# A norm's square sums are added up on ScalarE instead of GpSimd in a two-layer decoder trunk

## The chip, the core and the metric

The kernel runs on one core of a Trainium2 chip. The metric is the device time of one execution in microseconds. In the profile's names PE is TensorE (matmuls), PEld its weight loads, ACT is ScalarE, DVE is VectorE, POOL is GpSimd, and SP the engine that issues most transfers. Every engine works through its own queue in order; they meet at semaphores.

## The reference

A decoder trunk of two layers over 256 positions of width 1024, in float32. Each layer has four sublayers: a SwiGLU feed-forward block, a mixer (layer 0: a chunkwise mLSTM; layer 1: differential attention over a shared K and V), a second feed-forward block, and a gated input embedding. Each is wrapped in RMS norms before and after:

```python
def rms_norm(x, g):
    y = x * lax.rsqrt(jnp.mean(x * x, axis=-1, keepdims=True) + EPS)
    return y * g

h = swiglu(rms_norm(x, g[0]), w_ffn_in[layer, 0], w_ffn_out[layer, 0])
x = x + 0.5 * rms_norm(h, g[1])
h = mixer(rms_norm(x, g[2]))
x = x + rms_norm(h, g[3])
h = swiglu(rms_norm(x, g[4]), w_ffn_in[layer, 1], w_ffn_out[layer, 1])
x = x + 0.5 * rms_norm(h, g[5])
gate = sigmoid(rms_norm(x, g[6]) @ w_ple_gate[layer])
x = x + rms_norm((p[layer] @ w_ple_proj[layer]) * gate, g[7])
```

The time goes into the weight matrices: all of them are read once, and each product is made of three float32r matmuls with operands that are split into a high and a low part.

## The kernel before

The 256 positions are two tiles of 128 rows, t = 0 and 1. x lives in SBUF with a copy in HBM. A weight tile of 128x2048 (buffers `wraw`) comes in through SP's queue, ScalarE rounds it to its high part (`whi`), and VectorE subtracts to get the low part (`wlo`). The same split makes `xh` and `xl` of the transposed x and `hh` and `hl` of the hidden activations. PSUM has three banks `accI` for the products of the inner width, four `accO` for those of the outer width, and one `tr` for transposes.

The trunk is not issued in the order in which it is written. `Notes.add` (L123) records every operation with its dependences and a cost (`cost`, L212), and `play` (L267) lays the whole program out by a list schedule with these costs: for each engine it takes the operation that can start first, urgent ones ahead of the splits of weights, and for TensorE transposes only when their input has been ready for a margin of 300 ns (MARGIN). `issue` (L430) then emits all operations in that order, so that in the profile nearly every instruction has line L433. In the costs a two-input VectorE operation holds GpSimd back until it ends (L404 to L407), a GpSimd addition is 321 ns, a power 560 ns, and an ACTIVATE of one column with a bias by pointer 163 ns. A change of a few operations therefore changes the order of many others.

A norm has these parts. `squares` (L565) runs an ACTIVATE Square over 512 columns (256 in two places of the last sublayer) whose accumulator gives one column of a small tile `s2` of four columns; an ACTIVATION_READ_ACCUMULATOR belongs to it. `rnorm` (L570) adds the columns of `s2` and eps with tensor_scalar operations on GpSimd and calls `rpow` (L557), which raises the sum to the power -0.5 by a GpSimd tensor_tensor with the constant tile `mhalf`. There are two uses of the result. Behind a sublayer, `post` (L600) and the end of `ple` (L951) hand it to `add_to_x` (L589): VectorE multiplies the sublayer's output by it and adds it to x, two halves of 512 columns, and TensorE then transposes the new x (`pre`, L682). Ahead of a sublayer, `rms_x` (L668) takes the norm of x, and the result scales the products where they leave PSUM, as in `hidden` (L805). There are 32 such norms of one column per tile of positions: 31 over two square sums, and the very last one over three. The mLSTM's and the attention's own head norms use `rpow` or the power alone and have no `rnorm`.

The small tiles of one column (`sm`, L452) rotate through eight buffers, the waste tiles of the squares (`sg`, L459) through three that hold hidden activations too.

Of the kernel before, what the change touches and what calls it, by code (L numbers as in the profile page):

```python
# [12 lines left out]
AF = mybir.ActivationFunctionType  # L13
ALU = mybir.AluOpType
# [9 lines left out]
EPS = 1e-6  # L24
# [411 lines left out]
def trunk(nc, a):  # L436
    def T(shape, tag, bufs, dt=F32):
        return nc.tile("sb", shape, tag, bufs, dt)
# [13 lines left out]
    def small(cols=1):  # L452
        return T([P, cols], f"sm{cols}", {1: 8, 2: 4, 4: 16}[cols])
# [87 lines left out]
    make_identity(nc, ident)  # L541
    mhalf = T([P, 8], "mhalf", 1)
    nc.gpsimd.memset(mhalf, -0.5)


    nc.scalar.activation(small(), mhalf[:, 0:1], AF.Silu)
# [10 lines left out]
    def rpow(v, cols=1):  # L557
        r = small(cols)
        nc.gpsimd.tensor_tensor(r, v, mhalf[:, :cols], op=ALU.pow)
        return r  # L560
# [7 lines left out]


    def rnorm(s2, n, coef):  # L570
        v = small()
        nc.gpsimd.tensor_scalar(v, s2[:, 0:1], s2[:, 1:2], EPS / coef ** 2, op0=ALU.add, op1=ALU.add)
        for i in range(2, n):
            v2 = small()
            nc.gpsimd.tensor_scalar(v2, v, s2[:, i:i + 1], None, op0=ALU.add)
            v = v2
        r = rpow(v)
        return r

    def rms(srcs, coef):  # L580
        s2 = small(4)
        for i, src in enumerate(srcs):
            squares(src, coef, s2, i)
        return rnorm(s2, 2, coef)
# [15 lines left out]
    def post(t, srcs, gbc, coef):  # L600
        gbc, hg = gbc
        s2 = small(4)
        for i in range(2):
            squares(srcs[i], coef, s2, i)
            j = 1 - i
            nc.vector.tensor_tensor(hg[:, halves[j]], srcs[j], gbc[:, halves[j]], op=ALU.mult)
        add_to_x(t, hg, rnorm(s2, 2, coef))
# [316 lines left out]
    def ple(l, xts, rs, epilogue):  # L924
# [26 lines left out]
        def end(t, n):  # L951
            r = rnorm(s2[t], n, 1.0)
            add_to_x(t, hg, r, store if epilogue is None else None)
            if epilogue is not None:
                res.append(epilogue(t))
# [466 lines left out]
@with_exitstack  # L1422
def issue(ctx: ExitStack, tc: tile.TileContext, plan, a):
    pools = {
        "sb": ctx.enter_context(tc.tile_pool(name="sb", bufs=1)),
        "dr": ctx.enter_context(tc.tile_pool(name="dr", bufs=1, space=bass.MemoryType.DRAM)),
        "ps": ctx.enter_context(tc.tile_pool(name="ps", bufs=1, space=bass.MemoryType.PSUM)),
    }
    notes = Notes(tc.nc, pools, plan)
    trunk(notes, a)  # L1430
    with tc.manual_schedule():
        notes.issue()
# [69 lines left out]
```

## Time and profile before

| what | us |
|---|---|
| timed runs, median of 3 | 1003.71 (1002.12 to 1003.89) |
| profiled execution, its own time | 1002.59 |
| its span, first to last instruction | 1000.8 |
| TensorE's mean granted clock | 0.997 |
| GpSimd: 32 tensor_scalar of one column, busy | 23.5 |
| GpSimd: 32 powers of one column, busy | 21.9 |
| ScalarE: idle in the span (1000.8 less 698.6 busy) | 302.2 |

A row of the timeline gives the start within the span, the duration, the engine, the operation, what it writes and reads, how many like it were merged, and in brackets the idle time of the engine before it with what ended that. A row of groups gives the count, busy time, mean duration in ns, and the idle time before. A row of waits gives the total, the count, and the longest. A row of windows gives, for one stretch, each engine's busy time with its count of instructions, then the TensorE clock, the share of the DMA engines, and the rate.

### The profile page before, as it was taken

The page shows a single profiled execution, that of the slowest core. Times are in us where ns is not written, and L with a number is a line of the kernel's source. Part 1 is how long each engine was busy: PE and PEld are TensorE (multiplying, and loading weights), DVE is VectorE, ACT ScalarE, POOL GpSimd, SP SyncE. Part 2 cuts the span into 40 slices and gives each one's busy share as a digit, 9 for nine tenths or more (in the row PEclk, how much of TensorE's full clock was granted, in tenths as well). Part 3 has the DMA queues.
Part 4 walks back from the last instruction along what each step waited for, and adds up shares of the span by engine and source line. Part 5 has one row for each costly group of instructions (what it writes and reads, how often), then busy time and mean ns, then how long its engine had stood idle before and what let it go on. Part 6 is the DMA issues. An engine that isn't in the chain of part 4 may idle for free.

```text
span 1000.8 us, 12442 instructions
## 1 busy us (share of the span) xinstructions
PE 986.4 (99%) x4636; PEld 803.0 (80%) x4636; DVE 892.8 (89%) x909; ACT 698.6 (70%) x924; POOL 94.9 (9%) x126
## 2 busy tenths in 40 slices
PE   9999999999999999999999999999999999999997
PEld 7888888887787778888878888888888887878786
DVE  6977999799999999998799999898984999999983
ACT  7746777578756877685867767686776776757752
POOL 0010000300141000001120000001002300000010
PEclk9999999999999999999999999999999999999998
DMA  9999948765699999765699999864759899996621
GB/s 345 420 339 343 311 179 296 244 207 198 255 320 340 326 309 335 279 247 207 261 301 330 324 353 347 329 244 161 253 210 285 235 297 318 313 295 252 242 84 43
DMA packets 45859, 274.68 MB, mean 274 GB/s; under 512 B 5480, under 2 KB 5864, under 8 KB 16104
## 3 DMA queue, kind: packets, MB, share of 16 engines
q1 hardware_dynamic: 39752, 231.69, 60.2%
q0 software_dynamic: 5760, 41.95, 20.6%
q8 instruction: 36, 0.59, 0.2%
q10 hardware_dynamic: 288, 0.27, 0.1%
q14 instruction: 23, 0.19, 0.1%
HBM read 263.40 MB, written 10.49 MB: 274 GB/s over the span
## 4 chain that ended last, share of the span: by engine, by line
PE 47%; issue 2%; ACT 2%; POOL 1%; DVE 1%; DVEq 0%; POOLq 0%; ACTq 0%
PE accI L433 30%; PE accO L433 15%; PE tr L433 2%; POOL sm L433 1%; ACT sg L433 1%; DVE wlo_4r L433 0%; ACT att L433 0%; DVE wlo_2r L433 0%; ACT wraw L433 0%; ACT whi_5r L433 0%; ACT whi_0r L433 0%; DVE wraw L433 0%; DVE att L433 0%; DVE xl_5r L433 0%; DVEq L1498 0%
## 5 line engine op out<-in xcount | busy, mean ns | idle before, releaser
L433 DVE TENSOR_TENSOR wraw<-wraw,wraw 128x2048 f32<-128x2048 f32 x40 | 91.4, 2284 | 0.1
L433 ACT ACTIVATE whi_1r<-wraw 128x2048 fp32r<-128x2048 f32 (+2 forms) x49 | 72.7, 1494 | 18.2 <-PE accI L433 8.8
L433 ACT ACTIVATE whi_4r<-wraw 128x2048 fp32r<-128x2048 f32 (+1 forms) x45 | 75.4, 1684 | 11.9 <-issue 4.4
L433 ACT ACTIVATE whi_2r<-wraw 128x2048 fp32r<-128x2048 f32 (+1 forms) x48 | 79.4, 1661 | 5.5 <-issue 2.6
L433 ACT ACTIVATE whi_5r<-wraw 128x2048 fp32r<-128x2048 f32 (+1 forms) x47 | 79.2, 1694 | 5.6 <-PE accI L433 4.7
L433 ACT ACTIVATE whi_0r<-wraw 128x2048 fp32r<-128x2048 f32 (+2 forms) x48 | 74.5, 1557 | 6.8 <-PE accI L433 3.4
L433 ACT ACTIVATE whi_3r<-wraw 128x2048 fp32r<-128x2048 f32 (+1 forms) x45 | 73.6, 1647 | 3.3 <-PE accI L433 1.6
L433 ACT ACTIVATE att<-accI 128x512 f32<-128x512 f32 x80 | 47.5, 594 | 38.1 <-PE accI L433 37.8
L433 POOL DMA_DIRECT2D wraw<-in_ffn_in x36 | 32.0, 889 | 343.5 <-DMA wraw<-in_ffn_in 286.3
L433 POOL TENSOR_SCALAR sm<-sm 128x1 f32<-128x1 f32 x32 | 23.5, 735 | 308.8 <-ACT sg L433 308.8
L433 POOL TENSOR_TENSOR sm<-sm,mhalf 128x1 f32<-128x1 f32 (+2 forms) x40 | 30.7, 769 | 108.2 <-DVE sm L433 105.6
L433 ACT ACTIVATE sg<-att,sm 128x256 f32<-128x256 f32 x54 | 26.9, 502 | 16.9 <-DVE att L433 16.8
L433 ACT ACTIVATE sg<-accO 128x512 bf16<-128x512 f32 (+2 forms) x46 | 20.2, 445 | 25.0 <-PE accO L433 21.0
L433 ACT ACTIVATE sg<-accI,sm 128x256 f32<-128x256 f32 x34 | 16.0, 470 | 29.3 <-PE accI L433 27.3
L433 PEld LDWEIGHTS tr<-ident,sg 128*128 128x128 f32 x176 | 23.0, 140 | 14.6 <-DVE hl_2r L433 2.7
L433 PE MATMUL tr<-ident,sg 128*128 128x128 f32 x176 | 34.0, 274 | 0.3 <-DVE hl_2r L433 0.3
L433 DVE SCALAR_TENSOR_TENSOR wraw<-wraw,sm,wraw 128x512 f32<-128x512 f32 x32 | 22.7, 749 | 12.0 <-POOL sm L433 11.9
L433 DVE TENSOR_TENSOR att<-accI,att 128x512 f32<-128x512 f32 x40 | 27.4, 685 | 3.3 <-PE accI L433 2.9
L433 ACT ACTIVATE sg<-wraw 128x512 bf16<-128x512 f32 x32 | 20.1, 630 | 13.7 <-DVE wraw L433 9.7
L433 ACT ACTIVATE att<-accI,sm 128x512 f32<-128x512 f32 (+1 forms) x22 | 14.8, 671 | 20.8 <-PE accI L433 20.8
L433 DVE SCALAR_TENSOR_TENSOR sg<-att,sm,sg 128x256 f32<-128x256 f32 x54 | 25.7, 480 | 1.7 <-ACT sg L433 1.5
L433 DVE TENSOR_TENSOR att<-att,att 128x512 f32<-128x512 f32 (+1 forms) x33 | 22.4, 679 | 3.8 <-ACT att L433 3.6
(610 smaller groups left out, 3249.9 us busy)
## 6 DMA issues: line engine op xcount, KB each, us to landing
wraw<-in_ffn_in SPq DMA_DIRECT2D x102, 1024.0 KB, 9.4
wraw<-in_ffn_out SPq DMA_DIRECT2D x44, 1024.0 KB, 8.3
wraw<-in_ffn_in POOLq DMA_DIRECT2D x36, 1024.0 KB, 13.3
wraw<-in_mlstm_in SPq DMA_DIRECT2D x14, 1024.0 KB, 5.3
wraw<-in_ple_gate SPq DMA_DIRECT2D x8, 1024.0 KB, 5.1
wraw<-in_w_kv SPq DMA_DIRECT2D x8, 1024.0 KB, 4.8
home<-wraw SPq DMA_DIRECT2D x28, 256.0 KB, 5.1
wraw<-home SPq DMA_DIRECT2D x14, 512.0 KB, 5.4
```

The costliest lines, as they stand in the source:

```text
L433: getattr(getattr(self.nc, eng), name)(*args, **kw)
```

## The change

`rnorm` no longer uses GpSimd for sums. Two columns of `mhalf` that no power reads, 6 and 7, are overwritten with eps for the two coefficients. The sum then starts from eps, and each column of `s2` is added by an ACTIVATE Identity on ScalarE whose bias is the sum so far. The power stays on GpSimd.

```diff
     mhalf = T([P, 8], "mhalf", 1)
     nc.gpsimd.memset(mhalf, -0.5)
+    eps = {coef: mhalf[:, c:c + 1] for c, coef in ((6, 1.0), (7, 0.5))}
+    for coef, v in eps.items():
+        nc.gpsimd.memset(v, EPS / coef ** 2)
...
     def rnorm(s2, n, coef):
-        v = small()
-        nc.gpsimd.tensor_scalar(v, s2[:, 0:1], s2[:, 1:2], EPS / coef ** 2, op0=ALU.add, op1=ALU.add)
-        for i in range(2, n):
+        v = eps[coef]
+        for i in range(n):
             v2 = small()
-            nc.gpsimd.tensor_scalar(v2, v, s2[:, i:i + 1], None, op0=ALU.add)
+            nc.scalar.activation(v2, s2[:, i:i + 1], AF.Identity, bias=v)
             v = v2
-        r = rpow(v)
-        return r
+        return rpow(v)
```

A norm over two square sums so has one GpSimd operation less and two ScalarE operations more, and three small tiles in place of two. Since the schedule is made anew, the order of the other instructions changes too. Three places follow.

ScalarE at the first norm, right behind the first weight tiles; `sg` with `sm_0` or `sm_1` are the squares of x for t = 0 and t = 1, `sg_128<-accI_90` is the SiLU of the first hidden tile, which reads the norm's result. Before:

```order
L433 ACTIVATE sg_127,sm_0_134<-wraw_80 128x512
L433 ACTIVATE sg_128,sm_0_134<-wraw_80 128x512
L433 ACTIVATE sg_126,sm_1_135<-wraw_80 128x512
L433 ACTIVATE sg_127,sm_1_135<-wraw_80 128x512
L433 ACTIVATE sg_128<-accI_90,sm_2_158 128x256
L433 ACTIVATE whi_3r<-wraw_81 128x1024
```

Of the change:

```order
L433 ACTIVATE sg_127,sm_0_134<-wraw_80 128x512
L433 ACTIVATE sg_128,sm_0_134<-wraw_80 128x512
L433 ACTIVATE sm_1_157<-sm_0_134,mhalf_133 128x1
L433 ACTIVATE sg_126,sm_1_135<-wraw_80 128x512
L433 ACTIVATE sm_2_158<-sm_0_134,sm_1_157 128x1
L433 ACTIVATE sg_127,sm_1_135<-wraw_80 128x512
L433 ACTIVATE sm_4_160<-sm_1_135,mhalf_133 128x1
L433 ACTIVATE sg_128<-accI_90,sm_3_159 128x256
L433 ACTIVATE sm_5_161<-sm_1_135,sm_4_160 128x1
L433 ACTIVATE whi_3r<-wraw_81 128x1024
```

The second addition for t = 0 stands behind the first square for t = 1, and with it the power that it feeds.

ScalarE behind the second feed-forward block of layer 0, t = 0 (465 us in the profile), where `sg` with `sm_0` are the two squares of the block's output in the banks `accO`. Before:

```order
L433 ACTIVATE hh_1r<-tr_97 128x256
L433 ACTIVATE sg_128,sm_0_134<-accO_96 128x512
L433 ACTIVATE sg_126,sm_0_134<-accO_94 128x512
L433 ACTIVATE whi_0r<-wraw_79 128x1024
L433 ACTIVATE sg_127,sm_1_135<-wraw_76 128x512
```

Of the change:

```order
L433 ACTIVATE hh_1r<-tr_97 128x256
L433 ACTIVATE sg_128,sm_0_134<-accO_96 128x512
L433 ACTIVATE sm_0_156<-sm_0_134,mhalf_133 128x1
L433 ACTIVATE sg_126,sm_0_134<-accO_94 128x512
L433 ACTIVATE sm_5_161<-sm_0_134,sm_0_156 128x1
L433 ACTIVATE whi_5r<-wraw_78 128x1024
L433 ACTIVATE sg_127,sm_1_135<-wraw_76 128x512
```

The first addition stands between the two squares, the second behind both. So it is at 14 of the 16 norms behind a sublayer; at the other two, behind the second feed-forward blocks at t = 1, the two additions follow both squares.

VectorE behind the mLSTM's output projection, t = 1 (293 us in the profile): the two products with the norm's gains, subtractions of large weight tiles (`wlo`), and the addition to x (`wraw_80<-wraw_81,sm`). Before:

```order
L433 TENSOR_TENSOR wraw_81<-accO_93,wraw_81 128x512
L433 TENSOR_TENSOR wraw_81<-accO_95,wraw_81 128x512
L433 TENSOR_TENSOR wlo_2r<-wraw_82,whi_5r 128x2048
L433 TENSOR_TENSOR wlo_4r<-wraw_84,whi_2r 128x2048
L433 SCALAR_TENSOR_TENSOR wraw_80<-wraw_81,sm_2_158,wraw_80 128x512 x2
L433 SCALAR_TENSOR_TENSOR sg_127<-accI_90,sm_1_157,sg_127 128x256
```

Of the change:

```order
L433 TENSOR_TENSOR wraw_81<-accO_93,wraw_81 128x512
L433 TENSOR_TENSOR wraw_81<-accO_95,wraw_81 128x512
L433 TENSOR_TENSOR wlo_2r<-wraw_82,whi_5r 128x2048
L433 SCALAR_TENSOR_TENSOR wraw_80<-wraw_81,sm_4_160,wraw_80 128x512 x2
L433 TENSOR_TENSOR att_103<-tr_97,gcol_130 128x512
L433 TENSOR_TENSOR att_99<-accI_91,gcol_130 128x512
```

The addition to x now stands ahead of the second large subtraction, and TensorE's transposes of that x stand ten rows earlier in its order. The same happens behind the first feed-forward block of layer 0 and behind the attention, both at t = 1.

## The prediction

> **What bounds the kernel now.** I read the busy line of the page first, then who waited for whom, then the stretches in which TensorE lost time, then the norms one by one.
>
> ```profile
> PE 986.4 (99%) x4636; PEld 803.0 (80%) x4636; DVE 892.8 (89%) x909; ACT 698.6 (70%) x924; POOL 94.9 (9%) x126
> DVE wraw L433 <- POOL sm L433: 17.3, 20, 1.2
> PE tr L433 <- DVE wraw L433: 0.7, 2, 0.4
> 300.00:320.00 20.00, 18.88 (x86) 14.33 (x85) 19.83 (x25) 16.16 (x22) 2.68 (x4) 1.00 1.03 328
> 314.15 0.50 PE L433 MATMUL accI<-wlo_4r,xh_2r 128*128 128x512 f32 x1 [0.65 <-DVE wlo_4r L433]
> 831.23 0.50 PE L433 MATMUL accI<-whi_0r,xh_2r 128*128 128x512 f32 x1 [1.06 <-ACT whi_0r L433]
> 832.76 0.50 PE L433 MATMUL accI<-wlo_2r,xh_5r 128*128 128x512 f32 x1 [1.03 <-DVE wlo_2r L433]
> ```
>
> TensorE is busy 986.4 of 1000.8 us, so all its idle time together is 14.4 us. VectorE waits 20 times, 17.3 us in all, for GpSimd's norm results before it adds a sublayer's output to x; but TensorE's transposes of that x waited for VectorE only twice, 0.7 us together. The norm chain is therefore almost wholly hidden. What TensorE loses in mid-kernel it loses elsewhere: in stretches behind a norm such as 300 to 320, where VectorE is busy 19.83 of 20 us and the weights' halves come late (the waits at 314.15, 831.23 and 832.76). A shorter norm chain can win little; a longer one costs only where its cover is thinner than what it grows by. So I look at the cover, place by place.
>
> **The change part by part.** It removes 33 tensor_scalar from GpSimd and adds 65 one-column ACTIVATEs to ScalarE, one for every square sum, so two for most of the 32 norms. The power on GpSimd stays. The two new memsets fall before 18.50, the first norm, up to which GpSimd has nothing to do (its row below shows 17.20 us idle). No DMA is added or removed, and the count of table loads on ScalarE is 11 in both orders.
>
> Prices:
>
> ```profile
> L433 POOL TENSOR_SCALAR sm<-sm x32: 293/302/4202, 18.5 to 992.1; 128x1 f32<-128x1 f32 x32
> L433 ACT ACTIVATE sm<-mhalf 128x1 f32<-128x1 f32 x1 | 0.2, 203 | 0.0
> L433 ACT ACTIVATE att<-accI 128x512 f32<-128x512 f32 x80 | 47.5, 594 | 38.1 <-PE accI L433 37.8
> L433 ACT ACTIVATE att<-accI,sm 128x512 f32<-128x512 f32 x20 | 13.8, 691 | 18.8 <-PE accI L433 18.7
> ```
>
> A removed sum costs 0.30 us at its median. A one-column ACTIVATE without an operand by pointer takes 0.20; a pointer operand adds 691 - 594 = 97 ns at 512 columns, so one new addition takes 0.20 + 0.10 = 0.30. The same duration on either engine: the difference lies in where it stands. It is at least 0.20, and 0.39 if the pointer's step counted twice; the row with a pointer is the nearer. The 65 additions are 65 x 0.30 = 20 us on an engine that is idle for 300, and cost nothing where nobody waits behind them.
>
> *The first norm.* It is computed before the first hidden tile can be formed.
>
> ```profile
> 18.21 0.19 ACT L433 ACTIVATION_READ_ACCUMULATOR sg<-wraw 128x1 f32 x1
> 18.43 0.63 ACT L433 ACTIVATE sg<-wraw 128x512 bf16<-128x512 f32 x1
> 18.50 0.30 POOL L433 TENSOR_SCALAR sm<-sm 128x1 f32<-128x1 f32 x1 [17.20 <-ACT sg L433]
> 18.89 0.57 POOL L433 TENSOR_TENSOR sm<-sm,mhalf 128x1 f32<-128x1 f32 x1
> 18.96 0.19 ACT L433 ACTIVATION_READ_ACCUMULATOR sg<-wraw 128x1 f32 x1
> 19.06 0.62 ACT L433 ACTIVATE sg<-wraw 128x512 bf16<-128x512 f32 x1
> 19.67 0.46 ACT L433 ACTIVATE sg<-accI,sm 128x256 f32<-128x256 f32 x1
> 20.70 0.50 PE L433 MATMUL accI<-whi_2r,xh_1r 128*128 128x512 f32 x1 [0.16 <-DVE sg L433]
> ```
>
> Today the sum runs on GpSimd while ScalarE already squares the second token tile. In the new order the second addition of tile 0 stands behind the first square of tile 1. ScalarE starts an instruction 0.09 before the one ahead ends (the read of 18.96 ends at 19.15, the next starts at 19.06). So, from the read that ends at 18.40: first addition 18.31 to 18.61; square 18.52; second addition one square step (18.43 to 19.06, 0.63) later, 19.15 to 19.45; 0.16 to reach GpSimd (the hop from 994.86 to 995.02 in the tail's rows); power 19.61 to 20.18. ScalarE has then done the last square and the third addition and starts the SiLU at about 20.28 instead of 19.67. The gated tile and TensorE's next use of the bank follow it at a fixed distance, and TensorE was already waiting for them at 20.70. I charge **+0.6 us**. The order puts nothing else there that TensorE could do meanwhile.
>
> *The norms behind a sublayer, GpSimd free.*
>
> ```profile
> 464.47 0.60 ACT L433 ACTIVATE sg<-accO 128x512 bf16<-128x512 f32 x1 [0.26 <-DVE wraw L433]
> 464.96 0.20 ACT L433 ACTIVATION_READ_ACCUMULATOR sg<-accO 128x1 f32 x1
> 465.26 0.30 POOL L433 TENSOR_SCALAR sm<-sm 128x1 f32<-128x1 f32 x1 [79.17 <-ACT sg L433]
> 465.64 0.56 POOL L433 TENSOR_TENSOR sm<-sm,mhalf 128x1 f32<-128x1 f32 x1
> 466.24 1.41 DVE L433 SCALAR_TENSOR_TENSOR wraw<-wraw,sm,wraw 128x512 f32<-128x512 f32 x2 [1.21 <-POOL sm L433]
> 467.63 0.60 PE L433 MATMUL tr<-ident,wraw 128*128 128x128 f32 x4
> 777.27 1.42 DVE L433 SCALAR_TENSOR_TENSOR wraw<-wraw,sm,wraw 128x512 f32<-128x512 f32 x2 [0.61 <-POOL sm L433]
> 778.62 0.60 PE L433 MATMUL tr<-ident,wraw 128*128 128x128 f32 x4
> ```
>
> The new order sets the first addition between the two squares, into the 0.26 us that ScalarE waits there anyway; only the second stays in the chain. A GpSimd instruction that depends on the one before it starts 0.08 after that one ends (465.56 to 465.64); with that hop on ScalarE too: 465.16 + 0.08 + 0.30 + 0.16 = 465.70 against 465.64, **0.06 us later**. The first half of x is done at 466.24 + 0.75 = 466.99 (1.41 for two that overlap by the same 0.09: 0.75 each), and the transpose starts at 467.63: a cover of 0.64, and 0.60 by the second pair (778.02 to 778.62). Behind it stand other matmuls that need not wait. Cost **0**; without that cover it would be 0.06 each at seven such places, 0.4. Two additions stand side by side at two places only, one of them the norm of 471.82 below; there the chain grows by 0.06 + 0.38 = 0.44, but its sum took 0.85 today, 0.55 more than it needs, so that again nothing is lost.
>
> *The norms behind a sublayer, GpSimd held.*
>
> ```profile
> 293.97 4.20 POOL L433 TENSOR_SCALAR sm<-sm 128x1 f32<-128x1 f32 x1 [5.03 <-ACT sg L433]
> 295.80 2.28 DVE L433 TENSOR_TENSOR wlo_4r<-wraw,whi_2r 128x2048 fp32r<-128x2048 f32 x1
> 298.85 1.42 DVE L433 SCALAR_TENSOR_TENSOR wraw<-wraw,sm,wraw 128x512 f32<-128x512 f32 x2 [0.77 <-POOL sm L433]
> 299.23 0.39 PE L433 MATMUL accI<-wlo_2r,xh_5r 128*128 128x512 f32 x1
> 299.66 0.55 PE L433 MATMUL tr<-ident,wraw 128*128 128x128 f32 x3
> 505.91 0.65 PE L433 MATMUL tr<-ident,wraw 128*128 128x128 f32 x4 [0.23 <-DVE wraw L433]
> 471.82 0.85 POOL L433 TENSOR_SCALAR sm<-sm 128x1 f32<-128x1 f32 x1 [2.22 <-ACT sg L433]
> 472.51 1.22 DVE L433 TENSOR_TENSOR wlo_3r<-wraw,whi_0r 128x1024 fp32r<-128x1024 f32 x1
> 472.76 1.39 POOL L433 TENSOR_TENSOR sm<-sm,mhalf 128x1 f32<-128x1 f32 x1
> 474.18 1.42 DVE L433 SCALAR_TENSOR_TENSOR wraw<-wraw,sm,wraw 128x512 f32<-128x512 f32 x2 [0.45 <-POOL sm L433]
> ```
>
> Here the sum of 0.30 took 4.20: it came while VectorE subtracted two large weight tiles, both operands in SBUF, and ended 0.09 after the second one did. The power then still had to run, so VectorE stood 0.77. Where the power itself was held (472.76) VectorE stood only 0.45. With the sum on ScalarE the power is what meets the subtraction: 0.77 - 0.45 = 0.3 us sooner. The new order moreover lets the addition to x pass in front of one of the large subtractions, so that x is complete a whole subtraction (2.2 us) sooner, and the transposes stand ten rows earlier on TensorE; they meet x at about the same distance as now. TensorE lost 0.20 at 299.66 (a step of 0.43, where a matmul takes 0.23) and 0.23 at 505.91: 0.43 to be had at most, below that a loss of as much if the transposes now come too early. I take half as a gain, **-0.2 us**, since the 0.3 is nearer to removing a wait of 0.2 than to adding one.
>
> The Trainium skill (SBUF — State Buffer, "Who interferes with whom") says that the loser of the shared port between VectorE and GpSimd blocks until the other's instruction ends, with DVE-end + about 115 ns given for a descriptor write under "A bandwidth-pool intuition that's wrong". The 4.20 us row agrees with 0.09; the held power does not, it ended 0.42 after VectorE did (474.15 against 473.73). By the page the gain would be 0.3 more at each such norm and the term -0.4; by the row, -0.2. The same rule speaks against the change: the lock is not removed, only handed from the sum to the power.
>
> *The tail.*
>
> ```profile
> 994.67 0.19 ACT L433 ACTIVATION_READ_ACCUMULATOR sg<-att 128x1 f32 x1
> 995.02 0.29 POOL L433 TENSOR_SCALAR sm<-sm,sm 128x1 f32<-128x1 f32 x1 [2.64 <-ACT sg L433]
> 995.40 0.56 POOL L433 TENSOR_TENSOR sm<-sm,mhalf 128x1 f32<-128x1 f32 x1
> ```
>
> Nothing hides this one. Of its three additions only the last comes behind the last square: 994.86 + 0.08 + 0.30 + 0.16 = 995.40, where the power starts today: **0**, between -0.1 (no hop inside ScalarE) and +0.1 (a hop of 0.16 there).
>
> *Sum:* +0.6 + 0 - 0.2 + 0 = **+0.4 us**. The profiled execution took 1002.59 (span 1000.8 and 1.79 around it), so 1003.0 for one like it. The timed median, 1003.71, lies 1.12 above; the same +0.4 on it gives **1004.1**, inside what the measurement can tell from no change, about 0.2% or 2 us.
>
> **The rivals.**
>
> *Slower, VectorE kept waiting in front of a norm.* With the addition to x set ahead of a large subtraction, VectorE, which now fills that time with the subtraction, stands idle until the power is done, 0.45 by the row of 472.76 and up to 0.77 by that of 298.85. In stretches like that of 300 to 320 the weights then come later by as much, and TensorE waits at places like 314.15 and 832.76. At four such norms: 4 x 0.6 = 2.4, with the first norm's 0.6 1003.71 + 3.0 = 1006.7. It decides where VectorE's new idle time exceeds the 0.77 that it stood already; that today's wait is as long speaks against it.
>
> *Slower, the dependent addition waits long on its own engine.* No row shows ScalarE waiting for its own result. GpSimd's own hop is 0.08; 0.16 is the hop between engines. Each norm has two, so the chain grows by twice what lies above 0.08, and at the free norms it decides at a hop of 0.08 + 0.54 / 2 = 0.35. At 0.5 a chain grows by 0.84: 7 x 0.3 behind the cover, 0.8 at the first norm and 0.4 in the tail, 1004.1 + 3.3 = 1007.4. Two kinds of hop below 0.2 speak against it.
>
> *Faster, the held norms open up the busy stretches.* If x 2.2 us sooner lets TensorE fill the waits behind it, 0.43 + 0.65 + 1.06 + 1.03 = 3.2 go: 1003.71 + 0.6 - 3.2 = 1001.1. Against it: those waits are for subtractions and splits, whose number is unchanged.
>
> *The change does nothing:* excluded, the new order shows the additions.
>
> **How the numbers follow.** Forecast 0.60; VectorE waiting 0.16; own-engine hop 0.08; faster 0.16. The range runs from the faster case, 1001, to the slower ones, **1000.8 to 1007.5**; the re-laid plan moves thousands of TensorE rows by a place or two, which these ends also have to cover. Faster by over 0.2% (below 1001.7) 0.16, within 0.61, slower (above 1005.7) 0.23; the forecast's own spread is 1002.6 to 1005.6.
>
> **What would show it.** The wait of TensorE for the first hidden tile near 20.7 should grow to about 0.8 and everything behind it shift. Post norms should show one addition of 0.30 between the squares, VectorE's wait near 1.2 as before at free norms and 0.45 at held ones. If TensorE's transposes of x wait more than 0.7 in all, the cover was misread; if the waits at 314 and 831 to 833 gain or lose over 1 us, VectorE decided and not the chain. A new addition far from 0.30, or a gap over 0.35 between two, makes the prediction wrong.

## The result, and the profile after

| | us |
|---|---|
| kernel before, median of 4 runs beside it | 1003.06 (1002.12 to 1003.89) |
| changed kernel, median of 4 runs | 1010.33 (1008.17 to 1011.62) |
| ratio, 95% interval | 1.0073 (1.0059 to 1.0087) |
| predicted | 1004.1, range 1000.8 to 1007.5 |
| profiled execution of the changed kernel: time, span, mean granted clock | 1008.17, 1006.4, 0.998 |

The change costs 7.3 us, and the range did not hold it. The profiled execution is the shortest of the four, so its trace shows some 5.6 us of the loss; the rest comes up below (the clock).

Little of it is at the norms. First the page and the list of waits of the changed kernel (waits: total, count, longest).

```profile
PE 987.5 (98%) x4636; PEld 802.9 (80%) x4636; DVE 894.3 (89%) x909; ACT 713.7 (71%) x989; POOL 77.4 (8%) x95
DVE wraw L433 <- POOL sm L433: 16.3, 22, 1.2
PE tr L433 <- DVE wraw L433: 0.4, 1, 0.4
```

VectorE's waits for norm results went from 17.3 to 16.3 us, TensorE's for the new x from 0.7 to 0.4. Now the new additions by group, and a norm with GpSimd free, one with it held, and the tail, from the timeline of the changed kernel.

```profile
L433 ACT ACTIVATE sm<-sm,sm x33: 278/294/297, 18.9 to 1001.0; 128x1 f32<-128x1 f32 x33
L433 ACT ACTIVATE sm<-sm,mhalf x32: 278/284/296, 18.1 to 996.0; 128x1 f32<-128x1 f32 x32
```

```profile
467.79 0.20 ACT L433 ACTIVATION_READ_ACCUMULATOR sg<-accO 128x1 f32 x1
468.02 0.29 ACT L433 ACTIVATE sm<-sm,sm 128x1 f32<-128x1 f32 x1
468.46 0.56 POOL L433 TENSOR_TENSOR sm<-sm,mhalf 128x1 f32<-128x1 f32 x1 [81.03 <-ACT sm L433]
469.06 1.42 DVE L433 SCALAR_TENSOR_TENSOR wraw<-wraw,sm,wraw 128x512 f32<-128x512 f32 x2 [1.20 <-POOL sm L433]
470.23 0.60 PE L433 MATMUL tr<-ident,wraw 128*128 128x128 f32 x4
...
293.76 2.28 DVE L433 TENSOR_TENSOR wlo_2r<-wraw,whi_5r 128x2048 fp32r<-128x2048 f32 x1
294.37 2.08 POOL L433 TENSOR_TENSOR sm<-sm,mhalf 128x1 f32<-128x1 f32 x1 [6.67 <-ACT sm L433]
296.48 1.42 DVE L433 SCALAR_TENSOR_TENSOR wraw<-wraw,sm,wraw 128x512 f32<-128x512 f32 x2 [0.44 <-POOL sm L433]
297.34 0.60 PE L433 MATMUL tr<-ident,wraw 128*128 128x128 f32 x4
...
1000.78 0.19 ACT L433 ACTIVATION_READ_ACCUMULATOR sg<-att 128x1 f32 x1
1000.99 0.29 ACT L433 ACTIVATE sm<-sm,sm 128x1 f32<-128x1 f32 x1
1001.37 0.55 POOL L433 TENSOR_TENSOR sm<-sm,mhalf 128x1 f32<-128x1 f32 x1 [9.88 <-ACT sm L433]
```

An addition takes 0.28 to 0.30. It starts 0.02 to 0.03 after the end of the read that it depends on. At the free norm VectorE waits 1.20 (1.21 before) and x is done 0.42 ahead of its transpose; at the held one VectorE waits 0.44 (0.77 before); in the tail 0.40 pass from the read's end to the power, where 0.54 passed.

One cost at a norm remains, at the first. Here are the first square of x and the first SiLU that reads the norm, in the kernel before (its SiLU starts at 19.67 and the next matmul on that bank at 20.70, as the prediction's rows show) and in the changed one.

```profile
17.06 0.63 ACT L433 ACTIVATE sg<-wraw 128x512 bf16<-128x512 f32 x1 [0.22 <-DMA wraw<-in_x]
```

```profile
16.86 0.63 ACT L433 ACTIVATE sg<-wraw 128x512 bf16<-128x512 f32 x1 [0.22 <-DMA wraw<-in_x]
...
19.89 0.45 ACT L433 ACTIVATE sg<-accI,sm 128x256 f32<-128x256 f32 x1
```

From the square to the SiLU it is 2.61 before and 3.03 after: the additions cost 0.42 there.

The rest of the loss shows in TensorE's waits behind the norms, in the feed-forward blocks. Here are the large ones from the timeline of the changed kernel (the first row, 20.91, is the first norm's), then windows of before and of after (busy time of PE, PEld, DVE, ACT, POOL with counts, then TensorE's clock, the DMA share, GB/s).

```profile
20.91 0.50 PE L433 MATMUL accI<-whi_2r,xh_1r 128*128 128x512 f32 x1 [0.88 <-DVE sg L433]
314.50 0.50 PE L433 MATMUL accI<-wlo_3r,xh_2r 128*128 128x512 f32 x1 [0.83 <-DVE wlo_3r L433]
354.18 0.49 PE L433 MATMUL accI<-whi_3r,xh_5r 128*128 128x512 f32 x1 [1.24 <-ACT whi_3r L433]
355.10 0.50 PE L433 MATMUL accI<-wlo_2r,xh_0r 128*128 128x512 f32 x1 [0.42 <-DVE wlo_2r L433]
534.93 0.50 PE L433 MATMUL accI<-wlo_0r,xh_6r 128*128 128x512 f32 x1 [2.48 <-DVE wlo_0r L433]
838.14 0.50 PE L433 MATMUL accI<-whi_4r,xh_2r 128*128 128x512 f32 x1 [0.98 <-ACT whi_4r L433]
839.17 0.50 PE L433 MATMUL accI<-wlo_2r,xh_5r 128*128 128x512 f32 x1 [0.53 <-DVE wlo_2r L433]
```

```profile
340.00:360.00 20.00, 19.38 (x85) 15.17 (x84) 20.00 (x17) 13.07 (x14) 1.72 (x2) 1.00 0.96 329
520.00:540.00 20.00, 20.00 (x92) 16.34 (x91) 19.55 (x18) 12.15 (x12) 1.76 (x2) 1.00 1.00 367
```

```profile
340.00:360.00 20.00, 17.87 (x76) 13.51 (x75) 19.40 (x14) 14.30 (x15) 1.73 (x2) 1.00 0.95 317
520.00:540.00 20.00, 17.52 (x82) 14.03 (x81) 17.87 (x18) 10.05 (x11) 1.76 (x2) 1.00 1.01 398
```

In each of two stretches of 20 us TensorE does some ten matmuls fewer, waiting for weights (`whi`, `wlo`) that come late. The same can be read as a lag: how much later (us) the n-th matmul starts than the n-th of the kernel before, in the profiled executions (e1 to e9 are the experiments below; the 4636 matmuls are numbered in order of time, from 0).

```
n      before  after     e1     e2     e3     e4     e5     e6     e7     e8     e9
60       16.7  -0.50  -0.50  +1.04  -0.19  -0.41  -0.13  -0.31  -0.16  -0.36  -0.29
300      70.0  +0.19  -0.20  +1.11  -0.01  +0.10  +0.25  -0.15  -0.11  -0.04  +0.73
1200    261.2  +0.19  -0.17  +0.98  +0.10  -0.16  +0.08  -0.01  +0.16  -0.01  +8.29
1620    356.5  +2.86  +2.54  +1.00  -0.03  +2.17  -0.11  -0.19  +0.08  +2.67  +8.23
2400    526.1  +2.11  +2.24  +1.50  -0.76  +2.10  -0.36  -0.43  -0.38  +1.93  +8.46
2460    539.6  +4.84  +6.50  +1.50  +3.50  +2.13  -0.34  -0.40  +4.01  +2.44  +8.46
3120    685.9  +5.37  +7.24  +1.59  +3.66  +2.13  -0.37  -0.39  +4.26  +2.97  +8.42
3240    709.3  +6.67  +8.55  +1.50  +4.99  +2.10  +0.81  -1.39  +5.52  +4.25  +8.54
3720    792.7  +5.80  +8.09  +1.49  +4.16  +2.08  -0.01  -0.07  +4.69  +3.40 +10.47
3960    848.5  +6.42 +10.30  +4.08  +4.81  +3.66  +2.29  -0.11  +5.35  +4.14 +12.16
4635    993.1  +6.10  +9.90  +4.04  +4.39  +3.25  +1.91  -0.37  +4.93  +3.71 +11.80
```

Column "after": next to nothing until 261 us, 2.7 at about 350, 0.8 won back by 526, 2.7 at 535, and 1.3 in all behind that. The first row lies ahead of the first norm (18.5 us), so what stands there (1.04 in e2) is not the additions' doing.

### The profile page after: what moved, and what is told of

The parts are those of the page before. It is cut to its first block, busy times and chain, and to the rows that moved or that the text cites. A ratio compares the mean times of both kernels' runs of the same rounds, so it can differ in the third digit from the quotient of the medians.

```text
span 1006.4 us, 12473 instructions
## 1 busy us (share of the span) xinstructions
PE 987.5 (98%) x4636; PEld 802.9 (80%) x4636; DVE 894.3 (89%) x909; ACT 713.7 (71%) x989; POOL 77.4 (8%) x95
## 4 chain that ended last, share of the span: by engine, by line
PE 83%; DVE 6%; DMA 4%; ACT 3%; issue 2%; POOL 1%; SPq 0%; DVEq 0%; POOLq 0%; ACTq 0%
PE accI L433 49%; PE accO L433 30%; PE tr L433 4%; DMA wraw<-in_ffn_in 2%; DVE wraw L433 1%; DMA wraw<-in_mlstm_in 1%; ACT sg L433 1%; DVE att L433 1%; DVE wlo_2r L433 1%; DMA wraw<-in_x 1%; DVE wlo_0r L433 1%; POOL sm L433 1%; DVE wlo_3r L433 1%; DVE wlo_1r L433 1%; DMA wraw<-in_xT 1%
## 5 line engine op out<-in xcount | busy, mean ns | idle before, releaser
L433 ACT ACTIVATE whi_5r<-wraw 128x2048 fp32r<-128x2048 f32 (+1 forms) x45 | 75.6, 1681 | 14.3 <-PE accI L433 11.1
L433 ACT ACTIVATE whi_0r<-wraw 128x2048 fp32r<-128x2048 f32 (+2 forms) x51 | 79.9, 1573 | 3.9 <-DMA wraw<-in_ffn_in 2.6
L433 POOL TENSOR_TENSOR sm<-sm,mhalf 128x1 f32<-128x1 f32 (+2 forms) x40 | 39.4, 985 | 427.7 <-ACT sm L433 325.7
L433 ACT ACTIVATE hh_2r<-tr 128x256 fp32r<-128x256 f32 x28 | 10.7, 381 | 21.9 <-PE accO L433 15.3
```

The costliest lines, as they stand in the source:

```text
L433: getattr(getattr(self.nc, eng), name)(*args, **kw)
```

## The experiments

Theory A: the new order of the whole program costs the time, whichever engine adds. Theory B: the additions cost it, by stopping ScalarE. Each experiment also names **the planner's own length**: the latest end in the schedule that `play` lays with its own costs. It is 996.1 us for the kernel before and 1000.4 for the changed one. Norms are counted from 0 in the order of the calls of `rnorm`.

**Order and engine apart (e1, e2).** e1 keeps the changed kernel's order and exchanges the instructions where they are issued:

```diff
+            if nc.plan is not None:
+                nc.swap[len(nc.ops) - 1] = [] if i == 0 else [("gpsimd", "tensor_scalar", ...)]
```

> The order of every engine is that of the changed kernel, but each sum is added on GpSimd again: the first ScalarE addition of a norm is dropped, and the last one is replaced, at its place, by the old GpSimd instruction. Theory A (the new order of the whole program costs the time, whichever engine adds): within 1.5 us of the changed kernel, 1009 to 1011.5, with TensorE's waits near 345, 354 and 535 us still there. Theory B (the additions themselves cost it, by stopping ScalarE 65 times for about 0.3 us): back to about 1003.

Measured: 1010.71, ratio to before 1.0069 (1.0045 to 1.0094). That is the changed kernel's time, without one addition on ScalarE, and the waits near 345, 354 and 535 are there (0.46, 1.24 and 2.44). e2 is the reverse, the order of before with the additions set behind the squares:

```diff
+            for i in range(n):
+                at, v2 = squared[id(s2), i], s2[:, 3:4]
+                nc.swap[at] = [nc.ops[at], ("scalar", "activation", (v2, s2[:, i:i + 1], AF.Identity), dict(bias=v))]
+                v = v2
```

> The order of every engine is that of the kernel before, but each sum is added on ScalarE: the GpSimd sums are dropped, and each addition stands directly behind the square whose column it adds. Theory A (order): 1003 give or take 1.5, none of the waits near 354 and 535 us. Theory B (additions): 1008 to 1011.

Measured: 1005.51, ratio 1.0021 (1.0012 to 1.0031). The waits near 354 and 535 are not there. The additions cost something where no plan counted on them, 2 us over before, 1.0 beyond theory A's band of 1003 give or take 1.5. At the first norm, where each addition stands directly behind its square, it is 3.84 from the first square to the SiLU, against 2.61 before; in the profiled execution that falls together with a late start of TensorE (1.04 in the first row of the table). Another place, from the timeline of e2 around 800 us:

```profile
798.12 0.29 ACT L434 ACTIVATE sm<-sm,mhalf 128x1 f32<-128x1 f32 x1
...
799.06 0.29 ACT L434 ACTIVATE sm<-sm 128x1 f32<-128x1 f32 x1
...
800.78 0.37 ACT L434 ACTIVATE hh_0r<-tr 128x256 fp32r<-128x256 f32 x1
...
801.20 0.73 PE L434 MATMUL accO<-whi_0r,hh_0r 128*128 128x512 f32 x2 [0.55 <-ACT hh_0r L434]
```

`hh_0r` stands behind the two additions on ScalarE, 3.40 behind the first square of that norm (2.82 in the kernel before), and TensorE waits 0.55 for it. By the two, theory A carries the loss of 7.3; B is worth 2 at most, in another order.

**Which norm's new order (e3, e4).** In e3 and e4 a norm keeps GpSimd if its number is not in a set; the plan is laid anew.

```diff
+        norms.append(coef)
+        if len(norms) - 1 not in NEW:
+            v = small()
+            nc.gpsimd.tensor_scalar(v, s2[:, 0:1], s2[:, 1:2], EPS / coef ** 2, op0=ALU.add, op1=ALU.add)
+            ...
+            return rpow(v)
```

> All norms as in the changed kernel but one, number 8 counted from 0: the one behind the mLSTM's output projection for t = 1 (294 us), whose sum stays on GpSimd, and the planner lays everything out anew. If the loss between 296 and 375 us comes from what the planner does behind that one norm: 2.4 us less than the changed kernel, about 1008 (the planner's own length of its order goes from 1000.4 to 998.0). If the loss is spread over all norms: less than 0.4 us of change, about 1010.

Measured: 1005.84, ratio 1.0024 (1.0014 to 1.0034): 4.5 less than the changed kernel, where 2.4 was expected. The traces show less, a lag of 4.39 at the end against 6.10; the changed kernel's is its shortest run and has no halved clock, e3's has one (below).

> The other way round: only norm 8 (behind the mLSTM, t = 1) is added on ScalarE, the 31 others on GpSimd. If that one norm's new order costs the time between 296 and 375 us: 2.3 us more than the kernel before, about 1005.4 (the planner's own length goes from 996.1 to 998.4). If the loss is spread: 1003.2.

Measured: 1006.83, ratio 1.0035 (1.0022 to 1.0049): 3.4 more than the kernel before beside it (1003.48). In the table of lags e3 has nothing at 356 us and e4 has 2.2. The single norm brings the waits of the changed kernel with it, from the timeline of e4:

```profile
353.49 0.49 PE L434 MATMUL accI<-whi_3r,xh_5r 128*128 128x512 f32 x1 [1.24 <-ACT whi_3r L434]
354.41 0.50 PE L434 MATMUL accI<-wlo_2r,xh_0r 128*128 128x512 f32 x1 [0.43 <-DVE wlo_2r L434]
```

It is the norm of the prediction's row at 293.97, the one where VectorE's addition to x passes in front of a large subtraction. The addition to x starts 2.4 us sooner (296.48 against 298.85), and the price is paid 55 us later. The planner's own schedule shows it too: between 343 and 354 us TensorE waits 3.1 us in it for the changed kernel and for e4, and 1.3 for the kernel before, e3 and e5.

**VectorE's order there (e7).** All 32 norms on ScalarE, one rule more for the planner:

```diff
+    add_x = next(o for o in plan.ops if o.eng == "vector" and "sm1_543" in o.tiles)
+    big_lo = next(o for o in plan.ops if o.eng == "vector" and "wlo_582" in o.tiles)
+    add_x.after.setdefault(big_lo, False)
     plan.play(MARGIN)
```

> All 32 norms on ScalarE as in the changed kernel; the planner gets a single rule more, that at norm 8 VectorE's addition to x may not be set ahead of the second large subtraction, as it stood in the kernel before. If it is VectorE's order there that costs the time until 375 us: 1.9 to 2.7 us less than the changed kernel, with TensorE's waits of 1.4 and 0.7 near 354 gone, about 1008. If it is ScalarE's part (the additions behind the squares) or the earlier power: no change, 1010.3.

Measured: 1006.10, ratio 1.0025 (1.0014 to 1.0037), 4.2 less, more than the 1.9 to 2.7 expected. The rule caught only one of the two halves of the addition: the trace has one half ahead of the subtraction and one behind it. That was enough to end the lag at 356 us (0.08); other waits of TensorE took part of the place of the old ones (1.48 at 338 and 0.44 at 354). So VectorE's order at this norm carries the loss until 375, by way of the plan behind it; which of the later moves is needed for it was not tried.

**A second norm, and four (e5, e6).** The same code with two and with four numbers left out of the set:

```diff
-NEW = set(range(32))
+NEW = set(range(32)) - {8, 16}
```

> Two norms stay on GpSimd, the plan is laid anew: number 8 (behind the mLSTM, t = 1, 294 us) and number 16 (behind layer 0's input embedding, t = 1, 505 us). If the wait of 2.65 us near 532 that the kernel with norm 8 alone still has comes from what the planner does behind norm 16: that wait goes, and with it the 1.4 us of matmuls at half speed behind it, so 3 to 4 us below that kernel's 1005.8, 1002 to 1003. By the planner's own length (998.0 to 997.5) it would be only 0.5 less, 1005.3. If the wait at 532 has another cause: 1005.8.

Measured: 1003.31, ratio 0.9997 (0.9987 to 1.0006): level with before. Without the new order at two of 32 norms the whole loss is gone, and with 30 norms still added on ScalarE. The wait at 532 has vanished (lag -0.34 at 539.6), which the planner's own length, 0.5 less, did not show.

> Four norms stay on GpSimd (numbers 0, 8, 16, and 20, behind layer 1's first feed-forward block at t = 1, 705 us); the other 28 are added on ScalarE. If the loss sits at those four places and the ScalarE additions cost nothing elsewhere: the time of the kernel before, 1003.5 give or take 1.5 (the planner's own length is 996.2 against 996.1 there). If every addition on ScalarE costs a little: 28/32 of the changed kernel's loss, about 1009.

Measured: 1001.51, ratio 0.9978 (0.9968 to 0.9987). This version, 28 norms on ScalarE, beats both kernels and lies 0.5 below the expected band.

**One instruction (e8).** The wait of 2.48 at 534.93. Rows of ScalarE and VectorE ahead of it, from the timeline of the changed kernel:

```profile
507.71 0.45 SPq L433 DMA_DIRECT2D wraw<-in_ffn_in  x1
...
523.77 1.92 ACT L433 ACTIVATE whi_3r<-wraw 128x2048 fp32r<-128x2048 f32 x1 [2.81 <-DMA wraw<-in_ffn_in]
525.59 0.61 ACT L433 ACTIVATE xh_0r<-att 128x512 fp32r<-128x512 f32 x1
...
526.23 0.69 DVE L433 TENSOR_TENSOR xl_0r<-att,xh_0r 128x512 fp32r<-128x512 f32 x1 [2.13 <-ACT xh_0r L433]
...
532.58 2.29 DVE L433 TENSOR_TENSOR wlo_0r<-wraw,whi_3r 128x2048 fp32r<-128x2048 f32 x1
```

ScalarE stands 2.81 us for a transfer and then rounds for 1.92, with a short rounding behind it that becomes ready while it stands (by e8 below, at about 523). VectorE then stands 2.13 for that, and from 526.23 on works without a break up to the late `wlo_0r`. In the kernel before, the weight at this place came without a wait (518.74) and `xh_0r` at 521.05. The planner issued the transfer at 505.0 and counted on it at 517.8, 12.8 later; the chip issued it at 507.71 and ScalarE could start at 523.77, 16.1 later. In the planner's schedule TensorE waits 0.49 there.

```diff
     plan.play(MARGIN)
+    whi3, xh0 = [next(o.parts[0] for o in plan.ops if o.eng == "scalar" and v in o.tiles) for v in ("whi_1007", "xh_1044")]
+    plan.order.remove(whi3)
+    plan.order.insert(plan.order.index(xh0) + 1, whi3)
```

> The order of the changed kernel with one instruction moved: at 523 us ScalarE's rounding of a weight tile that still waits for its transfer (whi_3r, it stood 2.81 us for it) is set behind the short rounding of xh_0r instead of ahead of it. If TensorE's 2.64 us at 534.9 come from ScalarE standing for that transfer: VectorE's wait of 2.13 for xh_0r goes, the wait at 534.9 falls to 0.5 or less, and the time by 2 us, to about 1008. If the late weights themselves set it, or VectorE's backlog: the wait stays at 2.6 and the time at 1010.3.

Measured: 1006.89, ratio 1.0033 (1.0023 to 1.0043): 3.4 less than the changed kernel (2.4 in the traces: a lag of 2.44 against 4.84 at 539.6), for one of some 12,000 instructions moved. From its timeline:

```profile
522.96 0.63 ACT L433 ACTIVATE xh_0r<-att 128x512 fp32r<-128x512 f32 x1 [2.21 <-PE accI L433]
523.98 1.92 ACT L433 ACTIVATE whi_3r<-wraw 128x2048 fp32r<-128x2048 f32 x1 [0.38 <-DMA wraw<-in_ffn_in]
...
530.20 2.28 DVE L433 TENSOR_TENSOR wlo_0r<-wraw,whi_3r 128x2048 fp32r<-128x2048 f32 x1
...
532.54 0.50 PE L433 MATMUL accI<-wlo_0r,xh_6r 128*128 128x512 f32 x1 [0.27 <-DVE wlo_0r L433]
```

The weight is rounded no sooner (523.98 against 523.77), but `wlo_0r` is done 2.4 us sooner and TensorE waits 0.27.

**Nothing moved between engines (e9).** The kernel before, with one number of the planner changed:

```diff
-            o.dur = 560 if o.name == "tensor_tensor" else 320 + m
+            o.dur = 560 if o.name == "tensor_tensor" else 340 + m
```

> The kernel before with every instruction on the engine where it was; only the planner is told that a GpSimd addition takes 341 ns instead of 321 (the chip takes 300). If the time hangs on the order that the planner happens to lay: 2.9 us or more above the kernel before, 1006 to 1009 (the planner's own length goes from 996.1 to 999.1). If the engine that adds sets the time: unchanged, 1003.

Measured: 1010.64, ratio 1.0069 (1.0049 to 1.0089), above the 1006 to 1009 expected. Told that a GpSimd addition is 20 ns longer, the planner loses as much as by the change under study, and at another place, in the mLSTM. Its trace is the longest of its four runs (1014.51). Two waits and a halved clock behind the second make up 5.8 of the 6.9 us that the lag grows between 223 and 241 us of the kernel before. From the timelines of ScalarE and TensorE of e9:

```profile
226.41 0.50 PE L433 MATMUL accI<-whi_5r,xh_3r 128*128 128x512 f32 x1 [1.37 <-ACT xh_3r L433]
...
237.13 1.91 ACT L433 ACTIVATE whi_1r<-wraw 128x2048 fp32r<-128x2048 f32 x1 [5.10 <-DMA wraw<-in_mlstm_in]
238.94 0.58 ACT L433 ACTIVATE att<-accI 128x512 f32<-128x512 f32 x1
...
239.57 0.50 PE L433 MATMUL accI<-whi_4r,xh_4r 128*128 128x512 f32 x1 [2.79 <-ACT att L433]
```

It looks like the figure of e8 again: a large rounding stands 5.10 us for its transfer, and the short read of a PSUM bank that TensorE needs stands behind it. No run moved that one.

**Another draw for all three (e10, e11, e12).** The planner counts a transfer as landed `LATE` ns after its own estimate.

```diff
-LATE = 1000
+LATE = 650
```

> 28 norms on ScalarE, four (0, 8, 16, 20) on GpSimd, and the planner counts a transfer as landed 650 ns after its time instead of 1000. Its own length is 995.2, 1.0 less than the same split of the norms had with 1000 ns (which took 1001.5). If its length orders the kernels: 1000.5, the fastest of all. If the shorter allowance lets TensorE meet weights that have not landed: 1002 or more.

Measured: 1002.29, ratio 0.9992 (0.9982 to 1.0001): not the fastest. From the timelines of ScalarE and TensorE of e10:

```profile
336.24 0.38 ACT L434 ACTIVATE hh_1r<-tr 128x256 fp32r<-128x256 f32 x1
336.50 1.91 ACT L434 ACTIVATE whi_5r<-wraw 128x2048 fp32r<-128x2048 f32 x1
...
338.46 0.50 PE L434 MATMUL accI<-whi_5r,xh_1r 128*128 128x512 f32 x1 [2.18 <-ACT whi_5r L434]
```

The time is that of the second case, its reason is not: ScalarE begins `whi_5r` right behind `hh_1r`, with no idle time for a transfer, and the planner's own schedule has this wait too (2.34).

> All sums on GpSimd as in the kernel before, with the allowance of 650 ns. The planner's own length is 996.9, the same as that of all sums on ScalarE with this allowance. If the order is all that counts: 0.8 to 2 us above the kernel before, 1004 to 1005, and within 1.5 us of the kernel with all sums on ScalarE and 650 ns. If the additions on ScalarE cost by themselves: at least 4 us below that kernel.

Measured: 1008.84, ratio 1.0061 (1.0046 to 1.0076).

> The changed kernel, all 32 norms on ScalarE, with the allowance of 650 ns instead of 1000. The planner's own length falls from 1000.4 to 996.9. If the loss is the order's and not the additions': 1004 to 1005, 5 us or more below the changed kernel, level with all sums on GpSimd and 650 ns. If the additions cost: 1009 or more.

Measured: 1006.87, ratio 1.0040 (1.0027 to 1.0053). With this number the kernel with all sums on ScalarE is 2 us faster than the one with all on GpSimd, the other way round than with 1000. Both are some 2 us and more above what I expected, e12 is 3.5 below the changed kernel where 5 or more was expected, and the two lie 2.0 apart where 1.5 was the limit. A wait of 1.95 at 338 or 339 is in both traces, and the planner's schedules count it (2.11). They don't count the halved clock (two stretches in e11's trace, one in e12's), and of e12's wait of 2.58 at 533.88 they hold 0.49.

Where `LATE` is 1000, its own length orders the kernels fairly well (the kernel before took 1002.84 to 1003.48 beside the experiments):

| kernel | planner's own length | measured median |
|---|---|---|
| before | 996.1 | 1003.06 |
| e6, 28 norms | 996.2 | 1001.51 |
| e5, 30 norms | 997.5 | 1003.31 |
| e3, 31 norms | 998.0 | 1005.84 |
| e4, norm 8 alone | 998.4 | 1006.83 |
| e7, all, one rule | 998.4 | 1006.10 |
| e9, none, 20 ns | 999.1 | 1010.64 |
| changed kernel | 1000.4 | 1010.33 |
| e11, none, `LATE` 650 | 996.9 | 1008.84 |
| e12, all, `LATE` 650 | 996.9 | 1006.87 |
| e10, 28 norms, `LATE` 650 | 995.2 | 1002.29 |

## Why the prediction was wrong

- *A new addition 0.30.* Right: 0.28 to 0.30. *Own-engine hop 0.08.* It was 0.03, so that rival is out.
- *First norm +0.6.* The mechanism is right and the size is 0.42. From the first square of x to the SiLU it is 3.03 in all six traces with this order on ScalarE (after, e3, e5, e7, e8, e12) and 2.60 to 2.61 in the five with both tiles' sums on GpSimd (before, e1, e4, e9, e11). In all of them TensorE's matmul on that bank starts 1.02 to 1.03 behind the SiLU. That TensorE's wait came as said (about 0.8; 0.88 at 20.91) is luck: TensorE was 0.50 ahead of the kernel before at 16.7 us already. The same wait is 0.24 in e3 and 0.12 in e7 with the additions, and 0.62 in e4 and 1.03 in e9 without them.
- *Free norms 0, held norms -0.2, tail 0.* Right within 0.2 each, by the rows above, as far as waits show it. The power is indeed what now meets the subtraction, and VectorE's wait there is the predicted 0.45.
- *The slower rival, VectorE waiting in front of a norm add set ahead of a large subtraction.* It named the right place, norm 8, with the wrong mechanism: VectorE's wait fell there (0.77 to 0.44). And the waits that it said to watch hardly moved: 314 from 0.65 to 0.83, the pair of 831 to 833 from 2.09 to 1.51.
- **The step that failed** is the one sentence on the re-laid plan, that it "moves thousands of TensorE rows by a place or two", which the ends of the range "also have to cover". It was not a spread around the sum but its largest term: 2.7 us at about 350, 2.7 at 535, about 0.7 in the rest, and the clock. The prediction went through the new order at three places, next to the norms, and took the order elsewhere as of equal worth. e1 shows that the order alone costs all of it; e5 that the order behind two norms does; e9 that an order can cost as much when no instruction changes its engine.
- *"The new order moreover lets the addition to x pass in front of one of the large subtractions"* was read as a gain of 0.3. By e3, e4 and e7 this move is where the first 2.7 us start.

None of the prediction's own signs of being wrong showed (the additions, the gaps between them, the transposes' waits, the waits at 314 and 831 to 833): they watch the norms and two known waits, and the loss is elsewhere.

The planner's own length needs no run. It is no time on the chip (e10 to e12), but that it grew by 4.3 says that the new order was not of equal worth with the old. It foresees the waits at 345 to 355, and not the size of the one at 535 (0.49 in it, 2.48 measured).

## What to carry to other kernels

Where a planner lays the whole program anew, a change of a few operations is a new draw from its orders, and the draw can cost more than the operations. Try the operation and the order apart (new order with old instructions, and the reverse) before either is judged, and compare several draws. In an in-order queue, look for long work that waits for a transfer with short, ready work behind it: moving one such instruction gave back 2.4 us in the traces here, and 3.4 by the medians.

## What was not expected of the hardware

TensorE's granted clock falls to half for about 3.4 us behind some of these waits, and not in every execution. Windows of e3 behind its wait near 532, and of the changed kernel behind its wait at 534.93:

```profile
528.00:532.00 4.00, 1.56 (x7) 0.94 (x6) 4.00 (x5) 1.44 (x2) 0.00 (x0) 1.00 1.02 428
532.00:535.50 3.50, 3.46 (x8) 2.77 (x9) 3.50 (x3) 0.00 (x0) 1.20 (x2) 0.51 1.00 417
```

```profile
534.90:538.40 3.50, 3.47 (x16) 2.88 (x17) 3.50 (x3) 0.60 (x1) 1.74 (x2) 1.00 0.99 415
```

At clock 0.51 the stretch holds 8 matmuls, at 1.00 it holds 16. The profiled executions show it behind the wait near 535 in e1, e3 and e7, behind the pair of waits at 831 to 844 in e1, e2, e4, e5 and e9, behind the wait of 2.79 in e9, and behind waits at 338 to 357 in e11 (twice) and e12; the changed kernel's and before's do not show it while matmuls run. So waits of about 1.8 to 2.8 us, single or close together, can cost another 1.5 (eight matmuls at 427 ns instead of about 227). Others as long are not followed by it, such as e12's of 2.58 at 533.88. e1, with the changed kernel's order, has it at both places, a lag of 10.3 against 6.4 at 848.5 and a time of 1012.5. The halved clock is my reading of why the changed kernel's other three runs lie 2 to 3.5 us above the profiled one. It was not tried by itself, but the mean clock recorded for each run agrees. A stretch of 3.4 us at half takes 0.0017 off the mean over 1006 us; the profiled run has 0.998, the others 0.996, 0.996 and 0.995. Of e3's eight runs the four at 0.998 took 1004.5 to 1005.2, and the four at 0.996 took 1006.5 to 1006.7. The Trainium skill (TensorE: Matmul & The Clock Gate, "What's actually happening") has the clock at half after an idle window of about 3.4 us, counted by a window that runs free. The halving and the length agree with the row above; that 1.95 us of waiting is sometimes enough (e12, at 338) is shown here and not stated there.
